# A hybrid decoder layer: the accumulating transfers of the token mixer start at the receptances instead of at the first projection

## Chip, cores and metric

The kernel runs on one core of a Trainium2 chip. The metric is the device time of one execution in microseconds (us), lower is better.

## What is computed

One decoder layer on x of 512 tokens by 1024 channels, all in float32: a SwiGLU block, a token mixer with two branches, another SwiGLU block, and a last norm.

```python
def swiglu(x, w_gate, w_up, w_down):                       # d_ff = 2816
    return (jax.nn.silu(x @ w_gate) * (x @ w_up)) @ w_down

def token_mixer(h, w_in, ...):
    p = h @ w_in                                           # 42 x 128 columns
    pa, pb, pg = jnp.split(p, [COLS_A, COLS_A + COLS_B], axis=-1)
    b_gate, c_gate, u = jnp.split(pa, 3, axis=-1)
    y_a = (b_gate * causal_dwconv(c_gate * u, conv_w)) @ w_out_a
    pb = pb + (token_shift(pb) - pb) * mu_b
    r, k, v, xw, xa, xg = jnp.split(pb, SPLIT_B, axis=-1)
    ...                                                    # decay, iclr, gate, kk from these
    y = wkv7_scan(rh, heads(decay), kh, vh, -kk, kk * ah)  # 8 heads of 64, a delta-rule state
    ...                                                    # group norm, bonus
    y_b = (y * g) @ w_out_b
    g_a, g_b = jnp.split(pg, 2, axis=-1)
    merged = jax.nn.sigmoid(g_a) * y_a + jax.nn.sigmoid(g_b) * y_b
    return merged @ w_o

x = x + 0.5 * swiglu(rms_norm(x, ffn1_norm), ...)
x = x + token_mixer(rms_norm(x, mix_norm), ...)
x = x + 0.5 * swiglu(rms_norm(x, ffn2_norm), ...)
return rms_norm(x, final_norm)
```

## The kernel before

**Matmuls and weights.** Every float32 product is made of three matmuls of split operands (high and low part): whi·xhi, whi·xlo, wlo·xhi (`mm3`). Weights come in blocks of 128 x 1024 through one list, `stream`, in the order of use. For each block SyncE's queue issues a load into `raw`, ScalarE casts it to `whi`, VectorE makes `wlo` (raw minus whi), and `raw`, `whi` and `wlo` have four buffers each. One projection in the mixer (`project`, tile `ps_in`) takes one block and 24 matmuls, 8 channel tiles by 3.

**Sums of weights made in DRAM.** The down-projection of the first block and both projections of the second use a scheme with fewer products, which needs sums and differences of weight blocks. These sums are not made on an engine, but by transfers from DRAM to DRAM that GpSimd (POOL) issues, some of which add onto what lies at their destination (`accum_op`). `down_sums` and `up_sums` put them into one list, `queue`, by groups of 8 in a staggered order (`TURN`): four plain copies into f1, f3, f2, f4, then f1 and f3 get a second input added, then f2 gets f1 added, then f4 gets f2. There are 24 for the first down-projection (tiles `d1s`), 48 for the second up-projection (`us`) and 24 for the second down-projection (`ds`), 96 in all, most of 1 MB. A transfer that adds to or reads an earlier result has to wait until that has landed; the wait stands in POOL's own queue.

`step_sums(n)` (L575) takes the next n transfers from the list and records them at that point of the program. In the planner's eyes each depends on the operation recorded just before it; on the chip nothing but its place in POOL's queue and the landings that it needs hold it back. Steps are taken in the first up-projection (25), in the first down-projection (7), in the mixer (50), in the product with w_o (5), and in the second block (the rest).

**The mixer.** `MIXER` lists its steps in program order: `low` (decay and iclr), `key` 0, `conv` 0, `key` 1 to 3, `inv`, `conv` 1 to 3, `rec` 0 to 3 (receptances), `val` 0 to 3, `lg` (gate, low part), `pair` 0 to 3 (two heads each: the chunked state), with two `ga` between the first and the second half of the pairs, then the rest of the eight `ga` (gate of branch A and the product with w_out_a, tile `ps_oa`) and eight `gb`. A conv step makes three projections, a pair none, every other one makes one.

- `low` makes `sigw`, `iclr`, the scan `cum`, the exponentials `lam` and `ilam`, and `lamc`, a small VectorE copy of lam's chunk ends.
- `key` p: kk and its squares `sq`, `total` (cast `hi`, rest `lo`, two matmuls into `ps_sum`), root, reciprocal; `bh` = iclr·ilam on POOL; `ar` and one half of `bk` from kk on VectorE; on POOL `k` = k·iclr and the other half of `bk` from it.
- `inv`: 64 x 64 blocks of bk by ar (`ps_t`), copied to `dg`, transposed to `ln`; then the substitution, 31 steps of two VectorE operations (`tmp`, `wi`); two transpositions `uo` and `un`, and matmuls `ps_i` with them. The substitution's input is ready when `ln` is.
- `conv` p ends with a split into `chi` and `clo` (POOL), which `ga` reads.

**Who sets the order.** All operations are first recorded (a `Recorder` for each engine; some name several engines to choose from). Then `Plan.order` simulates the engines with a table of modelled costs (1500 ns on POOL for a transfer, its landing from 300 bytes a ns and 2 x 2 us, one after another) and gives each operation its engine and its place in that engine's queue: of the operations that are ready, the one recorded first goes first. So the recorded position of a transfer sets its priority and, through what it depends on, its earliest planned time; and each engine keeps the planned order on the chip.

Of the kernel before, what the change touches and what calls it, by code (L numbers as in the profile page):

```python
# [449 lines left out]
def layer_kernel(ctx: ExitStack, tc: tile.TileContext, xT, x, vecs, cst, gu1, dn1, win, wout, wo, gu2, dn2, lora, gateup, gmix, gff2, gfin, out):  # L450
# [20 lines left out]
    def psum(name="ps", shape=None):  # L471
        return Part(Slot(psp, shape or [P, S], F32, "ps", name))
# [102 lines left out]
    def step_sums(n=1):  # L575

        for _ in range(n):
            nxt = next(summing, None)
            if nxt:
                at = len(plan.ops) - 1  # L580
                nxt().deps.add(at)
# [44 lines left out]
    def weights(ahead=2):  # L626
        i = pos[0]
        pos[0] += 1
        for _ in make(i + 1 + ahead):
            pass  # L630
        w = made[i]
        made[i] = None
        return w
# [99 lines left out]
    def channels(xg, ps, w):  # L733

        cols = [(0, NQ)]
        if split_left[0]:
            split_left[0] -= 1
            cols = [(0, 2), (2, NQ)]
        for a, b in cols:
            cs_ = slice(a * P, b * P)  # L740
            for kt in range(KT):
                x = [t[:, kt].keyed([(q, kt // 4) for q in range(a, b)]) for t in xg]
                mm3(ps[:, cs_], w, x, sl(kt), cs_, kt == 0, kt == KT - 1)
# [284 lines left out]
    def project():  # L1028
        w = weights()
        ps = psum("ps_in")  # L1030
        channels(xg, ps, w)
        step_sums()
        return ps

    def shifted(i, name):
        ps = project()
        o = t2k(name)
        A.activation(out=o, in_=ps, func=AF.Identity, scale=omu[:, i:i + 1])
        V.scalar_tensor_tensor(out=o[:, 1:S], in0=ps[:, 0:S - 1], scalar=col("mu_b", i), in1=o[:, 1:S], op0=ALU.mult, op1=ALU.add)
        return o  # L1040
# [258 lines left out]
    def conv(p):  # L1299
        ps = project()  # L1300
        c_ = t2k("c")
        A.copy(out=c_, in_=ps)
        ps = project()
        cu = wide("cu")
        V.memset(cu[:, 0:2], 0.0)
        V.tensor_tensor(out=cu[:, 2:S + 2], in0=ps, in1=c_, op=ALU.mult)
        ps = project()
        o_ = t2k("conv")
        A.activation(out=o_, in_=cu[:, 0:S], func=AF.Identity, scale=col("conv_w", p))
        V.scalar_tensor_tensor(out=o_, in0=cu[:, 1:S + 1], scalar=col("conv_w", 4 + p), in1=o_, op0=ALU.mult, op1=ALU.add)  # L1310
        V.scalar_tensor_tensor(out=o_, in0=cu[:, 2:S + 2], scalar=col("conv_w", 8 + p), in1=o_, op0=ALU.mult, op1=ALU.add)
        V.tensor_tensor(out=o_, in0=o_, in1=ps, op=ALU.mult)
        hi = t2k("chi", dt=F32R)
        lo = t2k("clo", dt=F32R)
        A.copy(out=hi, in_=o_)
        G.tensor_tensor(out=lo, in0=o_, in1=hi.bitcast(F32), op=ALU.subtract)
        cv.append((hi, lo))
# [20 lines left out]
            "ga": gate_a, "gb": gate_b}  # L1338
    for what, i in MIXER:
        does[what](i)  # L1340
        if what == "pair":
            step_sums(2)


    ms = []
# [125 lines left out]
```

## Time and profile before

| | |
|---|---|
| median of 3 runs | 1145.55 us (1141.31 to 1150.65) |
| the profiled execution | 1142.87 us, of which the profile's span is 1141.1 us |
| PE, DVE, ACT, POOL busy | 97%, 67%, 49%, 27% of the span |
| first block, up and down | 0 to about 363 us |
| mixer: projections to gates | about 364 to 735 us |
| w_out_b, w_o | 735 to about 804 us |
| second block | about 804 to 1141 us |

PE is TensorE, DVE VectorE, ACT ScalarE, POOL GpSimd, SP SyncE; PEld is TensorE's loading of weights. "x<-y" names the tile written and the tiles read. Nearly every operation is recorded in one helper, so all have the same line, L437, and are told apart by their tiles. In a timeline a row gives start, duration, engine, operation and, in brackets, how long the engine had been idle before it and what ended that; "issue" there means that it waited for nothing the profile shows.

### The profile page before, as it was taken

To read this page: it belongs to the slowest core of one execution; us is meant where nothing else is said; L and a number is where in the kernel's file an instruction comes from. 1 tells how busy PE (TensorE), PEld (TensorE's weight loads), DVE (VectorE), ACT (ScalarE), POOL (GpSimd) and SP (SyncE) were. 2 spreads that over 40 slices of the span, in tenths; PEclk is the share of its full clock that TensorE was granted. 3 is DMA by queue.
4 is the path that set the end of the run, shared out by engine and by line. 5 is a ranking of instruction groups with operands and counts; after the bars stand their busy time and mean duration, and the time that the engine had idled before them with its cause. 6 is when DMAs were issued, how large, how long until landed. Compare 5 with 4: busy or idle time off the path is not lost.

```text
span 1141.1 us, 17088 instructions
## 1 busy us (share of the span) xinstructions
PE 1110.3 (97%) x6572; PEld 945.6 (83%) x6572; DVE 761.2 (67%) x1041; ACT 559.7 (49%) x964; POOL 305.3 (27%) x336
## 2 busy tenths in 40 slices
PE   8999999999999899989999999999999999999997
PEld 6888888888887777878777788888999999998886
DVE  5754454468867589995758742363987766768875
ACT  6422332236735776343655642333665555556744
POOL 4122121136840154234311121100011111217840
PEclk9999999999999989989999999999999999999999
DMA  8568686678899189889156679953576688875563
GB/s 307 171 221 222 239 219 197 177 189 278 282 296 362 43 193 280 232 237 256 53 139 180 154 226 330 306 179 116 174 221 248 213 216 271 229 246 185 190 190 119
DMA packets 67202, 244.87 MB, mean 215 GB/s; under 512 B 7089, under 2 KB 8113, under 8 KB 62129
## 3 DMA queue, kind: packets, MB, share of 16 engines
q1 hardware_dynamic: 48816, 151.51, 38.5%
q0 software_dynamic: 18304, 92.28, 32.4%
q8 instruction: 51, 0.84, 0.3%
q14 instruction: 31, 0.25, 0.1%
HBM read 237.47 MB, written 98.57 MB: 294 GB/s over the span
## 4 chain that ended last, share of the span: by engine, by line
PE 78%; DVE 8%; issue 6%; DMA 3%; ACT 2%; POOL 2%; SPq 0%; ACTq 0%; POOLq 0%; DVEq 0%
PE ps_gu L437 20%; PE ps_in L437 12%; PE ps_wx L437 11%; PE ps_dx L437 8%; PE ps_ww L437 5%; PE ps_o L437 4%; PE ps_dw L437 4%; PE ps_wc L437 3%; PE ps_dv L437 3%; PE ps_ob L437 2%; DVE wlo L437 2%; PE ps_oa L437 2%; DMA raw<-in_dn_dram 1%; DVE tmp L437 1%; PE ps_f L437 1%
## 5 line engine op out<-in xcount | busy, mean ns | idle before, releaser
L437 ACT CAST whi<-raw 128x1024 fp32r<-128x1024 f32 (+2 forms) x273 | 271.8, 997 | 441.8 <-issue 103.5
L437 DVE TENSOR_TENSOR wlo<-raw,whi 128x1024 fp32r<-128x1024 f32 (+2 forms) x273 | 333.6, 1228 | 184.1 <-ACT whi L437 178.5
L437 POOL TENSOR_TENSOR hp<-gg,hp 128x256 fp32r<-128x256 f32 x117 | 133.3, 1170 | 439.6 <-ACT hp L437 439.6
L437 PE MATMUL ps_gu<-xh,whi 128*128 128x512 f32 x352 | 137.1, 392 | 3.3 <-ACT whi L437 3.3
L437 PE MATMUL ps_in<-xl,whi 128*128 128x512 f32 (+1 forms) x360 | 137.5, 383 | 0.0
L437 PE MATMUL ps_in<-xh,wlo 128*128 128x512 f32 (+1 forms) x360 | 137.3, 382 | 0.0
L437 PE MATMUL ps_gu<-xl,whi 128*128 128x512 f32 x352 | 137.2, 391 | 0.0
L437 PE MATMUL ps_gu<-xh,wlo 128*128 128x512 f32 x352 | 137.2, 391 | 0.0
L437 PE MATMUL ps_in<-xh,whi 128*128 128x512 f32 (+1 forms) x360 | 137.0, 381 | 0.0
L437 PE MATMUL ps_dx<-whi,hp 128*128 128x512 f32 x352 | 112.8, 397 | 0.0
L437 PEld LDWEIGHTS ps_gu<-xh,whi 128*128 128x128 f32 x352 | 66.3, 188 | 18.6 <-ACT whi L437 4.6
L437 PEld LDWEIGHTS ps_dx<-whi,hp 128*128 128x128 f32 x352 | 66.6, 189 | 15.4
L437 PEld LDWEIGHTS ps_in<-xh,whi 128*128 128x128 f32 x360 | 68.2, 190 | 13.0 <-issue 0.4
L437 PEld LDWEIGHTS ps_in<-xl,whi 128*128 128x128 f32 x360 | 68.3, 190 | 12.6
L437 PEld LDWEIGHTS ps_in<-xh,wlo 128*128 128x128 f32 x360 | 68.2, 190 | 12.3
L437 PEld LDWEIGHTS ps_gu<-xh,wlo 128*128 128x128 f32 x352 | 66.6, 189 | 13.9
L437 PEld LDWEIGHTS ps_gu<-xl,whi 128*128 128x128 f32 x352 | 66.4, 189 | 13.8
L437 PE MATMUL ps_dx<-wlo,hp 128*128 128x512 f32 x176 | 69.8, 397 | 0.0
L437 DVE TENSOR_TENSOR uu<-ps_gu,rstd 128x512 f32<-128x512 f32 x22 | 15.2, 690 | 62.9 <-PE ps_gu L437 62.9
L437 PE MATMUL ps_dw<-whi,hp 128*128 128x512 f32 x176 | 55.6, 393 | 0.0
L437 ACT CAST hp<-gg 128x256 fp32r<-128x256 f32 x132 | 48.7, 404 | 13.1 <-DVE gg L437 13.0
L437 POOL DMA_DIRECT2D us<-in_gu_dram x36 | 30.7, 855 | 71.7 <-issue 60.4
(307 smaller groups left out, 2378.0 us busy)
## 6 DMA issues: line engine op xcount, KB each, us to landing
raw<-in_gu_dram SPq DMA_DIRECT2D x75, 512.0 KB, 4.1
us<-in_gu_dram POOLq DMA_DIRECT2D x30, 1024.0 KB, 9.5
raw<-us SPq DMA_DIRECT2D x44, 512.0 KB, 4.9
raw<-in_win_dram SPq DMA_DIRECT2D x42, 512.0 KB, 6.0
raw<-in_dn_dram SPq DMA_DIRECT2D x30, 512.0 KB, 4.7
d1s<-in_dn_dram POOLq DMA_DIRECT2D x12, 1024.0 KB, 8.3
ds<-in_dn_dram POOLq DMA_DIRECT2D x12, 1024.0 KB, 21.3
raw<-d1s SPq DMA_DIRECT2D x20, 512.0 KB, 6.4
```

Of the source, the lines that this page charges most:

```text
L437: return getattr(self.plan.engines[e], m)(**k)
```

## The change

`project()`, through which the 42 projections of the mixer go, no longer takes a step of the list. The loop over `MIXER` takes the steps instead: two after each receptance, value, the gate's low part and each pair (a pair had two before), and one and two in turn after the gates `ga` and `gb`. Nothing is taken in `low`, the keys, the inverse and the convolutions. The sum over the mixer is 50 as before, and the steps outside the mixer are untouched.

```diff
@@ -1029,7 +1029,6 @@
         w = weights()
         ps = psum("ps_in")
         channels(xg, ps, w)
-        step_sums()
         return ps
 
     def shifted(i, name):
@@ -1338,8 +1337,10 @@
             "ga": gate_a, "gb": gate_b}
     for what, i in MIXER:
         does[what](i)
-        if what == "pair":
+        if what in ("rec", "val", "lg", "pair"):
             step_sums(2)
+        elif what in ("ga", "gb"):
+            step_sums(1 + i % 2)
 
 
     ms = []
```

## Prediction

> **What bounds the kernel now.** I read the engine line of the page first, then the busy times by stretch of the mixer, then who waits for whom inside it.
>
> ```profile
> PE 1110.3 (97%) x6572; PEld 945.6 (83%) x6572; DVE 761.2 (67%) x1041; ACT 559.7 (49%) x964; POOL 305.3 (27%) x336
> q0 software_dynamic: 18304, 92.28, 32.4%
> ...
> 345.00:397.00 52.00, 48.12 (x295) 41.53 (x293) 32.38 (x46) 34.84 (x52) 3.06 (x4) 0.97 0.55 207
> 397.00:407.00 10.00, 5.21 (x14) 3.97 (x14) 8.63 (x8) 7.04 (x11) 6.51 (x7) 0.66 0.75 159
> 407.00:485.00 78.00, 77.39 (x447) 62.03 (x446) 72.57 (x103) 42.88 (x90) 32.20 (x33) 1.00 0.89 240
> 506.00:520.00 14.00, 13.34 (x279) 10.63 (x280) 12.83 (x32) 10.06 (x34) 9.33 (x15) 0.77 0.68 156
> 545.00:570.00 25.00, 22.48 (x253) 18.88 (x250) 19.33 (x53) 14.31 (x39) 8.22 (x22) 1.00 0.06 23
> 570.00:607.00 37.00, 35.55 (x234) 26.51 (x235) 24.56 (x39) 22.30 (x43) 4.28 (x5) 1.00 0.43 114
> 692.00:735.00 43.00, 43.00 (x191) 35.64 (x190) 10.49 (x9) 11.57 (x15) 5.43 (x8) 1.00 1.02 313
> 758.00:805.00 47.00, 47.00 (x218) 38.55 (x217) 20.54 (x32) 18.17 (x35) 0.00 (x0) 1.00 0.33 107
> ```
>
> The columns of a stretch are its length, then the busy time of PE, PEld, DVE, ACT and POOL, the granted clock, the DMA share and GB/s. PE is the bound: it is busy 1110.3 of 1141.1 us, so no change that leaves PE's work alone can bring more than 31 us. POOL, which the change relieves, is busy 27%. In the 78 us from 407 to 485, where most of the moved transfers run, PE is busy 77.39 and DVE 72.57: little idle time is left to win there. The weak places of the mixer's first half are 397 to 407 (PE 5.21 of 10.00, clock 0.66) and 506 to 520 (clock 0.77). The waits of PE from 345 to 735 say who made them:
>
> ```profile
> PE ps_sum L437 <- DVE hi L437: 5.0, 2, 4.8
> PE ps_i L437 <- DVE un L437: 3.8, 1, 3.8
> PE ps_sum L437 <- POOL lo L437: 0.2, 1, 0.2
> ```
>
> The two that lie ahead of the receptances' end, 5.0 and 3.8 us, are waits for DVE. POOL itself ended 0.2 us of PE's waits.
>
> **What is moved.** The 50 steps of the mixer stay 50. Before: 17 in low, the keys and the convolutions (1 + 4 + 12), 9 in receptances, values and the gate's low part, 8 in the pairs, 16 in the 16 gates. After: 0, 18, 8, 24 (per gate 1 and 2 in turn). So 17 issues leave POOL's queue ahead of the receptances; 9 come back up to the gate's low part and 8 in the gates. These are the first and the last of the 17, and the waits and instructions around them that matter:
>
> ```profile
> 341.70 0.70 POOL L437 DMA_DIRECT2D us<-in_gu_dram  x1 [7.30 <-issue]
> ...
> 395.32 1.30 POOL L437 TENSOR_TENSOR bh<-iclr,ilam 128x512 f32<-128x512 f32 x1 [44.21 <-issue]
> 396.57 1.17 POOL L437 DMA_DIRECT2D us<-in_gu_dram  x1
> 397.32 2.94 POOL L437 TENSOR_TENSOR bh<-iclr,ilam 128x512 f32<-128x512 f32 x2
> 399.78 1.70 POOL L437 TENSOR_TENSOR k<-k,iclr 128x512 f32<-128x512 f32 x1
> 404.97 1.20 POOL L437 DMA_DIRECT2D us<-us  x1 [3.49 <-issue]
> 405.73 1.90 POOL L437 TENSOR_TENSOR bk<-k,ilam 128x256 f32<-128x256 f32 x2
> 407.12 1.77 POOL L437 TENSOR_TENSOR bh<-iclr,ilam 128x512 f32<-128x512 f32 x1
> 416.70 1.16 POOL L437 DMA_DIRECT2D us<-in_gu_dram  x1 [7.81 <-issue]
> 417.44 1.74 POOL L437 TENSOR_TENSOR clo<-conv,chi 128x512 fp32r<-128x512 f32 x1
> ...
> 420.42 1.75 POOL L437 TENSOR_TENSOR k<-k,iclr 128x512 f32<-128x512 f32 x1 [0.56 <-ACT sq L437]
> ...
> 431.04 1.44 POOL L437 TENSOR_TENSOR lo<-sq,hi 128x512 fp32r<-128x512 f32 x1 [0.80 <-ACT hi L437]
> ...
> 454.67 0.96 POOL L436 MEMSET wi<- 128x1024 f32 x1 [6.79 <-DVE ln L437]
> ...
> 470.91 1.15 POOL L437 DMA_DIRECT2D us<-in_gu_dram  x1 [11.60 <-issue]
> 471.65 1.73 POOL L437 TENSOR_TENSOR clo<-conv,chi 128x512 fp32r<-128x512 f32 x1
> ...
> 484.13 0.71 POOL L437 DMA_DIRECT2D us<-in_gu_dram  x1 [2.05 <-issue]
> ...
> 587.41 1.16 PE ps_oa L437 x5
> ...
> POOL us L437 <- issue: 40.6, 8, 11.6
> ```
>
> **Their cost, if the order of everything else stayed.** An accumulating transfer waits in POOL's queue until the one it adds to has landed, and all of POOL stands behind it: 40.6 us in 8 waits from 396 to 485 (last row). That looks like the prize, and the chain of waits does lead through it. But I ask of each wait what stood behind it:
> - 3.49 us before 404.97: behind it the half of bk made of k, and the fourth bh. This half of bk is read first by the pairs, which come after all convolutions, receptances and values; that bh is key 3's, the last. Worth 0.
> - 7.81 us before 416.70: behind it clo, which the branch product reads from 587.41 on, and then k at 420.42, which idled another 0.56 us for ACT. Worth 0.
> - Up to 431.04: lo there waited 0.80 us for ACT after POOL was free. Worth 0.
> - Before the memset at 454.67, POOL idled 6.79 us for DVE's transposition. Worth 0.
> - 11.60 us before 470.91: behind it another clo. Worth 0.
>
> The issues themselves take 0.75 us of POOL each (396.57 to the next start, 397.32), 17 x 0.75 = 12.8 us, all inside this slack; at most the 0.2 us of PE's wait for lo hangs on them. Sum of this part: -0.2 to 0 us, taken as 0.
>
> **DMA load.** The weights' loads share the engines with the transfers. One transfer costs 0.324 x 1141.1 / 96 = 3.9 us of all 16 engines; 17 of them move 66 us from before 485 to after it. The three slack stretches above have 25 x 0.94 + 37 x 0.57 + 47 x 0.67 = 76 us free, so there is room. Relief in front is worth nothing as long as the loads wait for buffers, which they do:
>
> ```profile
> SPq L437 <- DVE wlo L437: 288.5, 47, 44.7
> ...
> raw<-us SPq DMA_DIRECT2D x44, 512.0 KB, 4.9
> ...
> 677.61 0.78 POOL L437 DMA_DIRECT2D us<-us  x1 [4.37 <-DMA us<-us]
> ...
> 809.24 9.95 SPq L437 DMA_DIRECT2D raw<-us  x4
> ...
> 1043.78 21.32 SPq L437 DMA_DIRECT2D raw<-ds  x10
> ...
> 840.54 0.92 POOL L437 TENSOR_TENSOR hp<-gg,hp 128x256 fp32r<-128x256 f32 x1 [106.78 <-ACT hp L437]
> ```
>
> 288.5 of the 390 us from 345 to 735 SyncE's queue waited for DVE to free a buffer. The crowding behind is covered too: from 692 to 735 the DMA share is full (1.02) and PE is busy 43.00 of 43.00, so a full DMA does not starve PE there. The last sum of the second up-projection is the 40th of the mixer's 50 transfers. It was issued at 677.61 with the sixth gate of branch A and now belongs to the second of branch B, four gates later; a gate of B has 24 matmuls and one of A 36, at 43.00 us for 191 of them 2 x 5.4 + 2 x 8.1 = 27 us, so about 705. The sums are first loaded at 809.24: 104 us of margin. Those of the down-projection are loaded from 1043.78. A backlog on POOL meets nothing before 840.54, where POOL had idled 106.78 us. Were this cover gone, each late load could stop PE for a landing of 4.9 us. Taken as 0.
>
> **The re-ordering.** What does change is the schedule. The kernel's planner fixes each engine's order by modelled times, and books 1.5 us of POOL per transfer: 17 x 1.5 = 25.5 us of planned POOL time go away ahead of the receptances, so the places of lo, bk, ps_t and ps_i in the queues may shift. The trace cannot show the new order; I bound it. At best both DVE stalls vanish with the slow clock behind them: 5.0 + 3.8, plus at most (1 - 0.66) x 10 = 3.4 and (1 - 0.77) x 14 = 3.2 us of clock: -15.4. At worst one stall of the longest kind (11.60) with its slow restart (3.4) is added: +15.0. I take -1 us: DVE, busy 72.57 of 78, sets the substitution's end in either order, so the nearest rows speak for a small effect; only the empty POOL speaks for a gain.
>
> **Sum.** 0 + 0 - 1 on the profiled execution's 1142.9 us gives 1142, and on the median of the runs, 1145.55, it gives 1144.5. I forecast **1143 us**, no change that can be told: about 1% (11.5 us) is what a measurement of this kernel can tell from none.
>
> **Rivals.**
> *The stalls go* (the substitution really starts earlier): the chain of waits speaks for it, the list of slack above against it. It would give 1143 - 15 = 1128 in full, some 1134 by half.
>
> *POOL's pauses were DVE's turn* (slower). At 395.73 three tiny copies stop DVE:
>
> ```profile
> 389.53 0.17 DVE L437 COPY lamc<-lam 128x8 f32<-128x8 f32 x1 [1.30 <-ACT lam L437]
> ...
> 395.73 5.87 DVE L437 COPY lamc<-lam 128x8 f32<-128x8 f32 x3 [1.82 <-ACT lam L437]
> ```
>
> One takes 0.17 us alone; three take 5.87 beside POOL's bh, bh, k, and end when POOL falls idle (399.78 + 1.70 = 401.48). DVE's cast to hi follows them in its order, and PE's 4.8 us stall waits for that. That idle time is the 3.49 us wait which the change removes. Without it bk, bk and bh (405.73 to 408.89) follow at once, DVE stays locked out 3.2 us longer, and the stall grows to 8.0: 1143 + 3 = 1146. It decides if POOL has those three ready at 401.48. The Trainium skill's page "SBUF — State Buffer", section "Who interferes with whom", states the rule that speaks against the change: such DVE copies and GpSimd instructions take one shared port pair, exclusively, for a whole instruction. The 5.87 us agree; by that rule the sum would be +3 instead of -1.
>
> *A wait on the path instead of off it* (slower, the larger one). From the first receptance to the last pair 26 transfers stand where 17 stood, between small POOL instructions that the values and pairs need soon:
>
> ```profile
> 515.52 1.95 POOL L437 TENSOR_TENSOR lo<-k,hi 128x512 fp32r<-128x512 f32 x1
> ```
>
> If a dependent transfer stands just ahead of such a lo, PE's ps_sum, next in PE's order, waits for a landing: 8 to 12 us (waits 7.81 and 11.60) and 3 of clock. One hit: 1155; two: over 1165. Against it: in before the same mixture cost PE only 0.2 us.
>
> **Chances.** The forecast, 1138 to 1150: 0.47. The longer lock-out, near 1146 and so in the same band: 0.15. The stalls gone, 1126 to 1137: 0.18, of it faster by over 1% (below 1134) 0.13. A wait on the path, 1151 to 1165: 0.20, of it slower by over 1% (above 1157) 0.12. The range takes in the band and reaches into both tails, 1130 to 1158, which leaves out about 0.17. Faster 0.13, within 1% 0.75, slower 0.12.
>
> **What would show it.** In the changed kernel no transfer stands between 350 and 485 and POOL's 40.6 us of waits there are gone; PE's idle time ahead of the receptances stays near 9 us; DVE stays over 90% busy from 407 to 485; the DMA share at 545 to 607 and 758 to 805 rises; PE stays full from 692 to 805. Wrong would be: PE's waits for hi and un gone (too pessimistic), lamc's copies longer than 5.87, or a PE wait for POOL of several us in values or pairs.

## The result: slower by 0.9%, and the profile after

The changed kernel takes **1157.28 us** (median of 4 runs, 1156.34 to 1159.19) beside 1145.66 for the kernel before in the same session: ratio 1.0093, 95% interval [1.0066, 1.0119]. I had forecast 1143. The profiled executions differ by 14.4 us of span (1155.5 against 1141.1). Here and below, ratios leave out the executions that ran slow (one each of e2, 2193 us, of e9, 6143, of e11, 1155, and of before, 1159), and medians take all.

Where those went is read from the starts of a few PE tiles in both traces. The stages are: start to the first `ps_in`; the front, to the first `ps_i`; receptances to gates, to the last `ps_in`; w_out_b and w_o, to the first `ps_wx`; the second up-projection, to the second block's first `ps_dx`; and the rest.

| us | start | front | receptances to gates | w_out_b, w_o | second up | rest |
|---|---|---|---|---|---|---|
| before | 363.8 | 142.7 | 228.5 | 68.8 | 223.3 | 114.0 |
| after | 365.4 | 137.1 | 238.7 | 68.7 | 231.5 | 114.1 |
| difference | +1.6 | -5.6 | +10.2 | -0.1 | +8.2 | +0.1 |

The start isn't touched by the change; over the profiled executions with that code it lies between 363.8 and 367.6. So there are three effects: the front **gained** 5.6 us, and two later places **lost** 10.2 and 8.2, together 18.4.

First the lines of the page that answer to those of before, then the same stretches (lengths, busy times of PE, PEld, DVE, ACT and POOL, clock, DMA share, GB/s), and PE's waits, in the mixer and then from 735 on:

```profile
PE 1116.8 (97%) x6572; PEld 950.2 (82%) x6572; DVE 762.2 (66%) x1040; ACT 558.4 (48%) x963; POOL 303.2 (26%) x336
```

```profile
397.00:407.00 10.00, 6.55 (x22) 4.93 (x21) 9.61 (x8) 9.70 (x16) 9.03 (x7) 0.83 0.04 11
407.00:485.00 78.00, 78.00 (x449) 62.70 (x449) 73.98 (x110) 42.46 (x89) 21.87 (x19) 1.00 0.32 100
...
545.00:570.00 25.00, 19.34 (x192) 16.16 (x191) 13.39 (x37) 10.45 (x30) 10.50 (x22) 0.86 0.87 225
...
692.00:735.00 43.00, 43.00 (x191) 35.54 (x190) 10.49 (x9) 11.87 (x15) 7.33 (x9) 1.00 1.00 284
758.00:805.00 47.00, 47.00 (x208) 38.17 (x208) 21.52 (x31) 16.43 (x28) 2.22 (x3) 1.00 0.87 275
```

```profile
PE ps_g L437 <- POOL lo L437: 5.0, 1, 5.0
...
PE ps_sum L437 <- DVE hi L437: 3.5, 1, 3.5
...
PE ps_i L437 <- DVE un L437: 1.6, 1, 1.6
...
PE ps_wx L437 <- ACT wq L437: 4.0, 2, 2.1
PE ps_ww L437 <- ACT wq L437: 2.8, 1, 2.8
```

PE's idle time grew by 7.9 us (1155.5 - 1116.8 against 1141.1 - 1110.3); the other 6.5 us are busy time, the same 6572 matmuls. Part of that is a lower clock behind the new stops (545 to 570: 0.86, 860 to 890: 0.94, both 1.00 in before). Another slow stretch stands behind no new stop of that length:

```profile
607.00:620.00 13.00, 9.49 (x75) 7.64 (x74) 12.30 (x33) 3.62 (x10) 1.15 (x1) 0.65 0.94 248
```

In before the clock there is 1.00; the longest stops around its start are 1.7 and 1.5 us now and 1.4 then. The two waits for DVE in the front shrank (5.0 to 3.5, 3.8 to 1.6). New are a wait of 5.0 us for POOL and, in the second up-projection, two of 2.1 and 2.8 us for ScalarE's `wq`, its copy of `ps_wx` or `ps_ww`. A third wait for `wq`, 1.95 us at 836.75, stands ahead of all transfers of that stage; before has it too (1.15 at 829.82, the 1.1 of its waits).

**The first loss.** POOL's and PE's timeline around that wait:

```profile
549.26 1.14 POOL L437 DMA_DIRECT2D us<-us  x1 [9.16 <-issue]
550.00 1.69 POOL L437 TENSOR_TENSOR lo<-lg,hi 128x512 fp32r<-128x512 f32 x1
```

```profile
551.74 0.79 PE L437 MATMUL ps_g<-lo,hi 128*128 128x512 f32 x1 [5.03 <-POOL lo L437]
```

A transfer that adds an earlier result stood 9.16 us in POOL's queue; one of the two issued just ahead of it, at 536.48, took 12.5 us and so landed at 549.0, right before it went. Right behind it stood the low part of the gate's `lg`, and PE's next matmul needed it.

**The second loss.** POOL at the start of the second up-projection, with the idle time ahead of `hp` (POOL's own arithmetic there), and what the transfers and loads issued there took to land (KB each, median us); then the same two views of before:

```profile
847.50 0.94 POOL L437 TENSOR_TENSOR hp<-gg,hp 128x256 fp32r<-128x256 f32 x1 [67.91 <-ACT hp L437]
849.81 1.48 POOL L437 TENSOR_TENSOR hp<-gg,hp 128x256 fp32r<-128x256 f32 x1 [1.38 <-ACT hp L437]
851.24 1.67 POOL L437 DMA_DIRECT2D ds<-ds  x2
852.32 1.43 POOL L437 DMA_DIRECT2D ds<-in_dn_dram  x1
```

```profile
raw<-in_gu_dram SPq DMA_DIRECT2D x3, 512.0 KB, 15.5
ds<-in_dn_dram POOLq DMA_DIRECT2D x1, 1024.0 KB, 22.6
raw<-us SPq DMA_DIRECT2D x2, 512.0 KB, 14.2
```

```profile
844.29 0.79 POOL L437 DMA_DIRECT2D ds<-ds  x1
...
858.95 0.57 POOL L437 DMA_DIRECT2D ds<-in_dn_dram  x1
```

```profile
raw<-in_gu_dram SPq DMA_DIRECT2D x6, 512.0 KB, 5.0
raw<-us SPq DMA_DIRECT2D x6, 512.0 KB, 4.1
```

Before, one transfer went out per step (j counts the steps of the second up-projection), the first two 14.7 us apart. After, three leave within 1.1 us: two that the planner had put behind `hp` in POOL's queue, although POOL stood idle for 67.91 us ahead of it, and the step of j = 0. The five loads issued behind them take 11.9 to 17.2 us; in before the medians are 4 to 5 and the slowest 9.4. ScalarE's casts wait for them:

```profile
ACT whi L437 <- DMA raw<-in_gu_dram: 11.5, 3, 4.3
```

`wq`, for which PE waits, stands behind those casts in ScalarE's queue.

### The profile page after: what moved, and what is told of

Read it like the earlier page. It is cut to its first block, busy times and chain, and to the rows that moved or that the text cites. A ratio compares the mean times of both kernels' runs of the same rounds, so it can differ in the third digit from the quotient of the medians.

```text
span 1155.5 us, 17074 instructions
## 1 busy us (share of the span) xinstructions
PE 1116.8 (97%) x6572; PEld 950.2 (82%) x6572; DVE 762.2 (66%) x1040; ACT 558.4 (48%) x963; POOL 303.2 (26%) x336
## 3 DMA queue, kind: packets, MB, share of 16 engines
q1 hardware_dynamic: 48816, 151.51, 38.6%
q0 software_dynamic: 18304, 92.28, 32.3%
## 5 line engine op out<-in xcount | busy, mean ns | idle before, releaser
L437 DVE TENSOR_TENSOR wlo<-raw,whi 128x1024 fp32r<-128x1024 f32 (+2 forms) x273 | 338.0, 1245 | 183.7 <-ACT whi L437 175.4
L437 PE MATMUL ps_gu<-xh,wlo 128*128 128x512 f32 x352 | 137.0, 391 | 0.0
L437 PE MATMUL ps_in<-xl,whi 128*128 128x512 f32 (+1 forms) x360 | 136.7, 380 | 0.0
L437 PEld LDWEIGHTS ps_in<-xh,wlo 128*128 128x128 f32 x360 | 67.9, 189 | 12.5
L437 DVE TENSOR_TENSOR uu<-ps_gu,rstd 128x512 f32<-128x512 f32 x22 | 15.2, 690 | 62.9 <-PE ps_gu L437 62.9
```

The lines of the kernel that those rows point to most:

```text
L437: return getattr(self.plan.engines[e], m)(**k)
```

## Experiments

My theories: **A**, the wait for `lg`'s low part makes the first loss; **C**, the three transfers at once make the second, because the loads behind them are late; **E**, the front's gain comes with the transfers' absence there. Rivals: the later mixer transfers as a whole make loads and clock worse, or the loss hangs on the place and not on the bunch. The edits are shown shortened: @@ names the place, helper functions are left out. All stages in one table, each from one traced execution:

| us | front | receptances to gates | second up | ratio to before, 95% |
|---|---|---|---|---|
| before | 142.7 | 228.5 | 223.3 | 1 |
| after | 137.1 | 238.7 | 231.5 | 1.0093 [1.0066, 1.0119] |
| e1: after, lg's low part on DVE | 138.4 | 230.7 | 232.3 | 1.0027 [0.9997, 1.0058] |
| e3: before, two steps moved to j = 0 | 143.1 | 235.7 | 224.1 | 1.0012 [0.9985, 1.0039] |
| e4: before, front's steps taken earlier | 136.7 | 229.2 | 224.2 | 1.0082 [1.0054, 1.0111] |
| e5: e1 without the bunch | 137.0 | 232.5 | 225.0 | 0.9987 [0.9965, 1.0009] |
| e6: before with a bunch of 3 | 142.6 | 228.5 | 224.1 | 1.0004 [0.9978, 1.0029] |
| e7: before, plain copies in front | 140.4 | 255.0 | 223.8 | 1.0163 [1.0116, 1.0211] |
| e8: after, spread anew | 135.8 | 229.8 | 238.4 | 1.0069 [1.0046, 1.0092] |
| e9: e8, w_o's steps moved later | 136.9 | 230.8 | 229.0 | 1.0025 [0.9998, 1.0052] |
| e10: before with a bunch of 5 | 143.2 | 228.5 | 229.1 | 1.0046 [1.0019, 1.0073] |
| e11: e9 with fewer pairs of steps | 136.7 | 229.2 | 225.8 | 0.9972 [0.9946, 0.9998] |

The middle column needs care. In e3 the steps of the mixer are those of before, and PE's waits behind the front too (`ps_tv` 2.5 and 1.2, `ps_y` 0.8), yet it took 7.2 us more: the granted clock fell in one execution and not in the other, without a longer stop. These are e3 and before:

```profile
620.00:650.00 30.00, 29.48 (x217) 23.89 (x218) 16.00 (x33) 15.08 (x38) 5.46 (x6) 0.72 0.89 208
620.00:650.00 30.00, 30.00 (x258) 22.94 (x258) 18.58 (x35) 20.02 (x47) 5.43 (x6) 1.00 0.85 197
```

So some 7 us in this column can be the clock alone; the ratios, over many executions, decide.

**e1: the lg part's low half on VectorE.**

```diff
-        lgs.extend((split(gw), split(lg)))
+        lgs.extend((split(gw), split_v(lg)))    # as split, lo on VectorE
```

> The changed kernel, with the rest lo of the gate's low part made on DVE instead of on POOL, where it stands behind a transfer that waits 9.16 us for a landing. Theory A (that one wait on the path costs the pairs their time: the stall of 5.03 us before ps_g at 551.74 and the slow clock behind it): ps_pq starts about 5 us after ps_tv's first, at some 552 instead of 555.6, and the end comes 4 to 8 us earlier, 1149 to 1153. Rival B (the pairs are slow because 26 transfers instead of 17 crowd POOL everywhere): the stall moves to another instruction and the time stays at 1156 to 1158.

1150.64 us. PE's row for the same matmul:

```profile
546.14 0.50 PE L437 MATMUL ps_g<-lo,hi 128*128 128x512 f32 x1 [0.57 <-DVE lo L437]
```

5.03 us became 0.57, the matmul took 0.50 instead of 0.79, and receptances to gates fell by 8.0 us; the ratios fell by 0.66%, some 7.6 us. A holds. How much of it is the stop and how much the clock is less sure: the stop gives 4.5 us and the clock from 545 to 570 an estimated (1 - 0.86) x 25 = 3.5, but the clock from 607 to 620 was 1.00 here too and 0.65 in the changed kernel, and some small waits grew. The bunch was still there (three issues from 844.71 to 845.79) and so was the second loss, 232.3.

**e2: after, w_o's five steps moved to the first up-projection.**

```diff
-                step_sums(2 if ft % 4 == 2 else 1)
+                step_sums(2 if ft % 2 == 0 else 1)
@@ w_o product
-            step_sums()
```

> The changed kernel, with the five steps of the product with w_o moved to the first up-projection, so that fewer transfers are left over for the second up-projection. Theory C (three transfers issued within 1.1 us at 851.24 starve the weight loads there, 12.1 to 17.3 us a load, and cost some 8 us): at most one or two transfers go out together after 840, no load of raw there takes over 8 us, the second up-projection takes 223 to 225 us instead of 231.5, and the time is 1148 to 1151. Rival D (the second up-projection is longer for another reason, the order or its own work): 1156 to 1158 still.

1157.93 us, ratio 1.0067 [1.0027, 1.0107], in the rival's range. **Inconclusive:** the trace shows that the bunch is gone (single transfers at 1606.79, 1634.77, 1662.86), but its stages can't be set beside the others', and the time mixes what the bunch's absence saves with what five more transfers cost the first block. By e4 below 17 more cost 16.3 us there, so five some 5, an estimate; the ratio's fall of 0.26% agrees with 8 saved and 5 paid, and shows neither.

**e3: before, with two of w_o's steps moved to j = 0.**

```diff
-            step_sums()
+            step_sums(1 if ft < 3 else 0)
@@ second up-projection
-                step_sums()
+                step_sums(3 if j == 0 else 1)
```

> The kernel before, with two of the five steps of the product with w_o moved to the first group of the second up-projection, which then takes three at once; the mixer's steps as before. Theory C (a bunch of three starves the loads there, whatever the mixer does): three transfers within about 2 us near 845, loads of 12 to 17 us behind them, the second up-projection 6 to 9 us longer, 1151 to 1155. Rival D: no change, 1144 to 1147.

1148.25 us, second up-projection 224.1. **Not a test of C:** the planner spread the transfers (853.15, 864.54, 867.40, 867.95), and no load took more than 10.5 us.

**e4: before, with the front's 17 steps taken in the first up-projection.**

```diff
-                step_sums(2 if ft % 4 == 2 else 1)
+                step_sums(3 if ft % 10 == 2 else 2)
@@ project
-        step_sums()
@@ loop over MIXER
+        elif what in ("rec", "val", "lg", "ga", "gb"):
+            step_sums()
```

> The kernel before, with the 17 steps of the low part, the keys and the convolutions moved to the first up-projection instead of to the steps behind; receptances to gates keep their one step, the pairs their two. Theory E (clearing the front in itself gains 4 to 6 us between the mixer's start and ps_i): from the first ps_in to the first ps_i 137 us instead of 142.8, and 1139 to 1142, if the first up-projection bears 17 more transfers. Rival F (the front's gain is not the transfers' absence but the accident of one order): 142 to 143 us there and 1144 to 1147, or more if the first up-projection suffers.

1155.23 us, above E's range. The front is 136.7 us: E holds without anything added later. But the first `ps_in` starts at 380.1 instead of 363.8. The transfers cost the first block 16.3 us, more than the front gains.

**e5: e1, and the bunch taken apart.**

```diff
@@ w_o product
-            step_sums()
+            step_sums(1 if ft < 3 else 0)
@@ second up-projection
-                step_sums()
+                step_sums(1 if j else 0)
```

> The changed kernel with both suspected losses taken away: the lg part's lo is computed by VectorE instead of GpSimd, and of the w_o product's five steps two are no longer issued there (only for ft < 3) and none at j = 0 of the second up-projection, so that in the planned order one transfer instead of three stands behind group 0's hp; the steps that are left over follow in the down-projection. Theory C (three transfers at once lengthen the loads that stand behind them to 12 to 17 us, and blocks that feed only 24 short matmuls cannot hide that): the second up-projection goes back to 224 +- 1.5 us, the wait for the lg part stays below 1 us, the front keeps its 137 to 138.5, and the kernel takes 1150.6 - 8 = 1142.5 us (1140 to 1145), 3 to 6 us less than before. Rival (the second up-projection is longer because the mixer's transfers as a whole come later, so that loads and clock are worse there): it stays at 231 to 232.5 us and the kernel takes 1149 to 1152 us.

1146.8 us. The second up-projection went from 232.3 to 225.0, as C said, and PE's waits for `wq` there from 6.0 to 2.2 us; the 2.2 stand at 833.22, ahead of the stage's transfers. The sum was expected 4 us too low: the start took 367.6 us, and receptances to gates 4.0 more than in before, with a clock of 0.64 from 607 to 620. The stop ahead of that, 1.73 us for DVE's `y`, is the same in e1, where the clock stayed at 1.00.

**e6: before with three transfers at once.**

```diff
-                step_sums()
+                if j == 2:
+                    bunch(3)       # three steps, one right behind the other
+                elif j > 2:
+                    step_sums()
```

> The kernel before with one thing added: in the second up-projection no step at j = 0 and 1, and at j = 2 three transfers issued one right behind the other; nothing else in the order changes. Theory C: the weight loads issued behind the three take 11 to 17 us instead of 4 to 5, the scalar engine's casts wait for them, TensorE stops for 3 to 6 us in all and its clock drops for a while; the second up-projection grows from 223.5 to 229 to 232 us and the kernel from 1146 to 1151 to 1155 us. Rival (the loads are lengthened but the buffers ahead hide it, the 8 us of the changed kernel come from somewhere else): TensorE's idle time there stays below 1 us and the second up-projection at 223 to 225 us.

1146.1 us: **no effect, C in that form is wrong.** The bunch was there, the loads behind it were late, and PE hardly noticed (one stop of 0.45 us at 895.38):

```profile
874.85 0.80 POOL L437 DMA_DIRECT2D ds<-ds  x1
875.40 1.33 POOL L437 DMA_DIRECT2D ds<-in_dn_dram  x2
```

```profile
raw<-us SPq DMA_DIRECT2D x4, 512.0 KB, 10.3
```

These three have 1024, 768 and 768 KB, those of the changed kernel 3 x 1024, and the loads took 8.5 to 10.8 us instead of 11.9 to 17.2. That suggested a cover: `raw` has four buffers and loads follow each other every 2.86 us there (853.55, 856.39, 859.26), so a load may take about 4 x 2.86 = 11.4 us before it is late, an estimate.

**e10: the same with five**, to test the cover.

```diff
-                if j == 2:
-                    bunch(3)
-                elif j > 2:
+                if j == 4:
+                    bunch(5)
+                elif j > 4:
```

> The kernel before with one thing added: in the second up-projection no step at j = 0 to 3, and at j = 4 five transfers issued one right behind the other (4.1 MB; the bunch of three had 2.5 MB). Theory (what counts is how long the loads behind them take, against a cover of 10 to 12 us): the loads take 14 to 18 us, TensorE stops for 3 to 7 us in all, the up-projection grows from 224 to 229 to 233 and the kernel from 1146 to 1150 to 1155 us. Rival (the changed kernel's loss hangs on the place, the up-projection's start, and not on the landing): TensorE stops for less than 1 us and the kernel takes 1145 to 1148 us.

1151.51 us, second up-projection 229.1. The slowest load and PE's waits:

```profile
raw<-in_gu_dram SPq DMA_DIRECT2D x1, 512.0 KB, 13.4
```

```profile
PE ps_ww L437 <- ACT wq L437: 2.5, 1, 2.5
PE ps_wx L437 <- ACT wq L437: 1.9, 2, 1.1
```

One of the three waits, 1.1 us at 831.44, is the one at the stage's start; 0.82 and 2.51 stand at 941.48 and 947.10, behind the bunch. So it is the landing time and not the place. Loads were a little less late than expected (9.7 to 13.4 for 14 to 18), the time fell into the range.

**e7: before, with only plain copies in the front.** The 17 places stay, but what waits for a landing is taken at the pairs and gates.

```diff
-        step_sums()
+        (step_plain if front[0] else step_sums)()
@@ loop over MIXER
+        elif what in ("ga", "gb"):
+            step_sums(1 + i % 2)
```

> The kernel before, with 17 transfers left at their places in the front (low, key, conv, inv), but only such as wait for no landing (plain copies); the accumulating ones follow at the places of the pairs and gates. So GpSimd's landing waits in the front (40.6 us) go, its 17 issues and the DMA traffic stay. Theory E1 (the landing waits on GpSimd make the 5.7 us that the changed kernel's front is shorter): the front, from the first ps_in to the first ps_i, falls from 142.7 to 136.5 to 138.5 us. E2 (the 1.5 us that the planner books for each issue, and the order that follows from it, or the DMA traffic make it): the front stays at 141.5 to 143.5 us. By either, the kernel's end depends on where the accumulating ones come to stand: by E1 1139 to 1146 us, by E2 1144 to 1152 us.

1166.63 us, outside both expectations. POOL's waits for landings from 345 to 485 fell from 48.0 us in 9 to 10.0 in 2, and the front to 140.4, between the two theories: 2.3 of the 5.6 us went with these waits, though the order changed with them; the rest hangs on the issues, the order or the traffic, which I haven't separated. The loss is A's mechanism in a larger size, as more dependent transfers stand together behind the front. Three waits of POOL, 8.48, 6.66 and 7.12 us, stand ahead of `lo`; these are the last of them and PE's row:

```profile
564.79 1.15 POOL L437 DMA_DIRECT2D us<-in_gu_dram  x1 [7.12 <-issue]
566.01 1.26 POOL L437 TENSOR_TENSOR lo<-lg,hi 128x512 fp32r<-128x512 f32 x1
```

```profile
567.32 0.79 PE L437 MATMUL ps_g<-lo,hi 128*128 128x512 f32 x1 [16.12 <-POOL lo L437]
```

**e8: a new spread.** Front free; one step per receptance, value and lg, one more per step of the w_out_b product, none at j = 0; the planner books transfers with 500 bytes per ns.

```diff
-        if what in ("rec", "val", "lg", "pair"):
+        if what == "pair":
             step_sums(2)
+        elif what in ("rec", "val", "lg"):
+            step_sums()
```

> A version made from the theories: as in the changed kernel no transfer from the low-rank parts to the substitution, but after that one step per receptance, value and lg part, two per pair, one or two per gate, one more per step of the branch product, and none at j = 0 of the second up-projection; and the planner books a transfer with 500 instead of 300 bytes per ns, which is nearer to the landings of the traces. Theories A and C: front 137 to 138.5 us, no wait over 1.5 us of TensorE for GpSimd in the values and pairs, no three transfers at once at the second up-projection's start (223 to 225.5 us), and 1139 to 1144 us in all. Rival (what the front gains is given back wherever the transfers are put, since their landings always meet something): 1146 to 1154 us, with a new wait for GpSimd or a load in the pairs, gates or up-projection.

1155.12 us, just past the rival's range. The front (135.8) came out a little better than expected, and in the pairs PE waited 1.1 us for POOL; the loss moved to the first loads of the second up-projection:

```profile
792.17 0.83 POOL L437 DMA_DIRECT2D ds<-in_dn_dram  x1 [6.30 <-issue]
798.19 0.81 POOL L437 DMA_DIRECT2D ds<-ds  x1 [5.20 <-DMA ds<-ds]
```

```profile
raw<-us SPq DMA_DIRECT2D x2, 512.0 KB, 15.7
raw<-in_gu_dram SPq DMA_DIRECT2D x1, 512.0 KB, 18.0
```

```profile
PE ps_wc L437 <- ACT whi L437: 9.0, 1, 9.0
```

The backlog landed until 818, and the three loads issued from 803 on stood beside it.

**e9: w_o's five steps go to the second up-projection**, none at j = 0 and 1, two at 2, 4, 6, 8, 9 and 10, one at 3, 5 and 7.

> The previous version (no transfers in the front, spread after it, transfers booked at 500 bytes per ns) with one difference: the five steps of the w_o product are not issued there but as second steps in the second up-projection, at j = 2, 4, 6, 8 and 9. Theory (a weight load is late only where it is issued behind three or more outstanding transfers; up to some 10.8 us of landing are hidden): the transfers are through before the second up-projection's first loads, those take 4 to 6 instead of 14 to 18 us, TensorE's 9.00 us stop there goes, the second up-projection takes 223 to 226 us instead of 238, two transfers per step lengthen loads to 7 to 10 us without a stop over 0.5 us; 1138 to 1145 us, 2 to 9 less than before. Rival (the transfers left for the up-projection cost there as much as they do elsewhere): 1148 to 1155 us.

1150.5 us, in the rival's range; half of the theory held. The 9.0 us stop went, but two transfers beside a rest of the ones before made a load of 14.1 us, and PE waited 3.7 us for `wq` at 936.23. The up-projection took 229.0 instead of 223 to 226.

**e11: two of w_o's steps back, one per j from 1 to 7, two at 8, 9, 10.**

> The version before (e9) with the steps once more apart: the w_o product issues two of its five again (ft < 2), and the second up-projection one per step from j = 1 to 7 and two only at j = 8, 9 and 10. Theory (loads up to some 11 us are hidden, from 12 us on they stop TensorE): no load there takes over 11.5 us, the stop of 3.68 us at j = 6 goes, the second up-projection takes 223.5 to 225.5 us instead of 229, and the kernel 1150.5 - 4.5 = 1146 us (1141 to 1148): the front's 6 us are kept only in part, since the pairs take 2 us more and its clock is lower. Rival (the extra transfers cost the up-projection about 5 us wherever they stand): 1149 to 1152 us.

1142.95 us, second up-projection 225.8. The slowest load and the only wait over 0.4 us:

```profile
raw<-in_dn_dram SPq DMA_DIRECT2D x1, 512.0 KB, 11.5
```

```profile
PE ps_wx L437 <- ACT wq L437: 1.9, 1, 1.9
```

The wait stands at the stage's start, 828.28, behind no late load. The loads of 11.5 are blocks of the down-projection; among the up-projection's own the slowest took 10.5. This version is faster than the changed kernel, and by 0.28% [0.02%, 0.54%] than the one before, which is barely clear of the noise. All stops against the slowest load near them:

| | slowest load, us | PE's stops behind it, us |
|---|---|---|
| e11, up-projection's own | 10.5 | none over 0.4 |
| e6 | 10.8 | 0.45 |
| e10 | 13.4 | 0.8 + 2.5 |
| e9 | 14.1 | 3.7 |
| e1 | 16.6 | 1.5 + 2.7 |
| after | 17.2 | 2.1 + 2.8 |
| e8, at the stage's start | 18.0 | 9.0 |

The limit lies between 10.8 and 13.4 us; no run places it closer. At all of these stops but e8's PE waits for `wq` behind a cast that waits for its load, so with `wq` ahead of that cast in ScalarE's queue the same load might cost less. No run tried that.

## Why the prediction was wrong

**"A full DMA does not starve PE" was a rule of another stage.** This step set late loads to 0, and it lost 8.2 us. It still holds where I read it: from 692 to 735 PE is busy 43.00 of 43.00. In before the loads there were nearly as late (up to 15.2 us) as in the second up-projection of after (up to 17.2), and harmless:

```profile
raw<-in_wout_dram SPq DMA_DIRECT2D x4, 512.0 KB, 12.7
...
raw<-in_win_dram SPq DMA_DIRECT2D x1, 512.0 KB, 15.2
```

One block feeds 24 matmuls there, 43.00 x 24 / 191 = 5.4 us, and four buffers would cover some 21 us, an estimate that no load there came up to; in the second up-projection a block lasts 2.86 us and they cover some 11.4. I worked out how much DMA time is free, not how late a load may be.

**"A backlog on POOL meets nothing before 840.54"** was right in time (the last of the backlog was issued at 778.76) and wrong in order. The planner believes transfers to land one after another at 300 bytes per ns, so it placed two of w_o's behind `hp` of 847.50, and they met the first step of the up-projection. The last sums of the second up-projection, too, left at 739.35 and not at about 705 as I had worked out, since POOL's waits for landings had grown; here the margin held, as the stage starts at 809.9.

**"A wait on the path instead of off it", given 0.20, is what happened**, on the `lo` of `lg` and not of the values. Its price was 8 to 12 and 3 of clock; the wait of 9.16 on POOL cost PE 5.03, and e1 puts the whole at some 8 us. "In before the same mixture cost PE only 0.2 us" was no argument against it: from 485 to 735 POOL's waits of that kind had 34.9 us in 7, and now have 128.4 in 19.

**The re-ordering, taken as -1,** was -5.6 in the front. DVE did stay at 73.98 of 78 busy, as predicted, but I had called all slack worth 0 and left PE's 9 us ahead of the first `ps_i` untouched (4.79 + 0.44 + 3.77); 5.0 were left (3.45 + 1.56), and a higher clock (397 to 407: 0.83, was 0.66) gave most of the rest. e4, e5, e8, e9 and e11, each without transfers in the front, have 135.8 to 137.0, and e1 has 138.4. By which path the two waits shrank is open: e7 gives 2.3 us to POOL's waits and leaves the rest undivided.

**"POOL's pauses were DVE's turn" is refuted.** In the changed kernel POOL ran four bh without a pause, beside them the three copies:

```profile
396.81 5.00 POOL L437 TENSOR_TENSOR bh<-iclr,ilam 128x512 f32<-128x512 f32 x4 [63.74 <-ACT ilam L437]
```

```profile
397.22 3.39 DVE L437 COPY lamc<-lam 128x8 f32<-128x8 f32 x3 [1.80 <-ACT lam L437]
```

They took 3.39 us instead of 5.87, not 8 or more, and ended at 400.61 while POOL worked on to 401.81. The Trainium skill's "SBUF — State Buffer", section "Who interferes with whom", still agrees in kind (3.39 / 3 = 1.13 us for a copy that takes 0.17 alone, about one turn for each POOL instruction of 5.00 / 4 = 1.25); what failed was my reading that DVE gets its turn only when POOL falls idle.

**Right:** no transfers from 350 to 485 (the first goes out at 489.60), a DMA share of 0.87 from 758 to 805, PE full from 692 to 805, and the sign that I had named for being wrong, a wait of several us for POOL in the pairs. The time lies inside the range by luck: its upper end was drawn for that rival, nothing in the working foresaw the second loss, and the front's gain hid nearly a third of both.

## What to carry to other kernels

In this kernel a load could be late by about as much as its buffers cover, number of buffers times the time that one block feeds the engine, and this is another number in each stage: ask of moved traffic how long a load behind it takes, not only whether the DMA engines have room. An instruction that waits in a queue costs what stands directly behind it, so a dependent transfer belongs behind work that nobody waits for, and its place must be read from the queue's order, since a planner with too slow a model of landings puts transfers behind instructions that come late.

## What the runs showed of the hardware

- Transfers from DRAM to DRAM of 1 MB that are issued together delay each other and the loads: the three of 851 to 853, two that add and a plain copy, landed 11.3, 16.9 and 22.6 us after issue, while in before a single one that adds took 11.1 and plain ones of 768 KB 5.2. A load of 512 KB beside them went from 4 or 5 to 12.1 us for the first and 17.2 for the third. The Trainium skill's "DMA: Bandwidth & Descriptors", section "Queues, rings and completion order", says that each DMA engine takes turns between queues, packet by packet. By the mean sizes in the profile of before (92.28 MB in 18304 packets for POOL's queue, 151.51 MB in 48816 for SyncE's) a load would then get 3.1 of 8.1 parts, 38%, and take 11 to 13 us, an estimate that takes the profile's packets for that section's. The first load's 12.1 agrees; but from 853 to 872 SyncE's queue moved 1.29 of 4.31 MB, 30%, so the loads got less than that.
- A stop of PE costs more than its length: in the changed kernel the matmul behind the 5.03 us took 0.79 us, in e1 behind 0.57 us the same matmul took 0.50.
- The granted clock also falls in some executions and not in others behind the same short stops: e3 from 620 to 650 0.72 where before has 1.00, e5 from 607 to 620 0.64 where e1 has 1.00. What decides it, no run here shows.
